# A decoder layer's mixer output projection: column blocks taken in pairs, with seven products in three of eight chunk pairs

## The chip, the cores and the metric

The kernel runs on one NeuronCore of a Trainium2 chip. Its time is the device time of one execution in microseconds. Work is spread over TensorE (PE, matrix products; its weight loads are listed as PEld), VectorE (DVE, elementwise), ScalarE (ACT, casts and activations), GpSimd (POOL, some elementwise work and a DMA queue) and SyncE (SP, the queue that loads the weights).

## The reference

One decoder layer on 256 tokens of width 2048, all in float32:

```python
x = x + 0.5 * swiglu(rms_norm(x, g1), w_gate, w_up, w_down)          # width 5632
h = rms_norm(x, g2); p = h @ w_in
merged = gate_attn * (y_attn @ w_proj_attn) + gate_rwkv * (y_rwkv @ w_proj_rwkv)
x = x + merged @ w_out                                               # 2048 x 2048
x = x + cross_attention(rms_norm(x, g3), rms_norm(mem, g4))          # 256 memory rows
x = x + 0.5 * swiglu(rms_norm(x, g5), ...)
return rms_norm(x, g6)
```

`y_attn` is a sliding-window attention, `y_rwkv` an RWKV-7 recurrence. The change lies in the line `x = x + merged @ w_out`.

## The kernel before, in words

**Float32 in two parts.** A matmul operand v is split into a rounded part `hi` (float32r) and the rest `lo = v - hi`. A product is three matmuls: hi·hi, hi·lo and lo·hi (`times`, L413 to L419). Activations are split once. Weights are split as they come: `load` (L321) brings a unit (two chunks of 128 rows by 512 columns, 512 KB) on SyncE's queue, `split_unit` (L338) casts `hi` on ScalarE (L344) and subtracts `lo` on VectorE (L345). In the mixer the raw weights have four buffers of one unit (tag `raw` of the pool `w`); in the feed-forwards they come in double units from a pool of their own, eight units ahead. `hi` and `lo` have three buffers each.

**Single blocks and pairs.** `product` (L399) computes one column block of 512: for each unit 12 matmuls (two chunks, two halves of the tokens, three parts). `product_pair` (L474) computes two column blocks together, one *item* (two units, one of each block) at a time. Over two chunks and two token halves these are eight products. In some items they become seven, by combinations in the manner of Strassen and Winograd: of the weights (L371 to L374, four subtractions into two further tiles, which `two_parts`, L348, splits into `thi` and `tlo`) and of the activations (`combinations`, L428: `chi` and `clo`). The sums then come out as p1 to p7 in banks of PSUM: p6 and p7 in the two banks that transposes use (`tr`), p1, p3, p5 in `mm`, p2, p4 and a further q in `acc`. The caller's `first`, `middle` and `out` combine them. The feed-forwards use pairs: (0, 2, 4) of eight items in gate and up, (2, 4, 6) or (2, 4) in down (`SEVEN`, `SEVEN_DOWN`). The mixer and the cross-attention use single blocks.

**Order of the work.** The weights come in the order of `weight_plan` (L97). `next_item` (L376) loads and divides an item and those after it, up to two units ahead (`AHEAD`). Side work is written as generators in an `Interleave` (L52): groups such as `feat` (transposes of a finished block and its split), `chain` (the recurrence), `norm`, `ew` and `mem`; each `tick` between products takes a step of each group. A scheduler then orders each engine's instructions by its own planned times, and adds waits on buffers.

**The stages around the change.** For each of four column blocks the kernel multiplies `yr` by `w_proj_rwkv` (L1394 to L1402); VectorE multiplies by the gate (`gl`, L1400), GpSimd adds the attention's share (`ml`, L1401), and `merged` transposes and splits the block into `mt`. Then the output projection (L1414 to L1424): for each block `product(mt, w_out)`, VectorE adds to the residual `x2` (L1421, read from `x1d` by GpSimd's queue, L1418), and the norm of that block (`n3.block`, L633) is spawned. Beside it `memory` (L1407) loads four blocks of the memory (L1410), and norms and transposes them. All the mixer's larger tiles share a ring of 23 (`t4`); the recurrence's smaller tiles (`xs`, `p`, `d`, `sm`, `yq`, `nt`, `bk`, `sq`) lie beside it in the same pool `mx` until the mixer ends.

Of the kernel before, what the change touches and what calls it, by code (L numbers as in the profile page):

```python
# [7 lines left out]
F32 = mybir.dt.float32  # L8
# [7 lines left out]
P = 128  # L16
# [21 lines left out]
SEVEN, SEVEN_DOWN = (0, 2, 4), ((2, 4, 6), (2, 4))  # L38

# [93 lines left out]
def decoder_layer(ctx: ExitStack, tc: tile.TileContext, a: dict, out: bass.AP):  # L133
# [185 lines left out]
    at = {"item": 0, "product": 0, "pool": None}  # L319
# [28 lines left out]
    def two_parts(v, e):  # L348
        sp = at["pool"]
# [3 lines left out]
        dve.tensor_tensor(lo[:], v[:], f32(hi[:]), ALU.subtract)  # L353
        return hi, lo

    def divide(i):
# [13 lines left out]
        t = [wp.tile([P, KU, 512], F32, tag="raw", name="raw", bufs=4) for _ in range(2)]  # L370
# [58 lines left out]
    def combinations(sp, x: Act, seven, name, ready=lambda: True, early=True):  # L429
# [8 lines left out]
        def work():  # L438
# [3 lines left out]
            for q in pairs:  # L442
                while not {2 * q, 2 * q + 1} <= x.done:
                    yield
                t = wp.tile([P, KU, 512], F32, tag="raw", name="raw", bufs=4)
# [31 lines left out]
    def product_pair(x: Act, c, w, first, middle, out):  # L477
# [28 lines left out]
        for q in range(nk // KU):  # L506
            k = KU * q
            if q in seven:
                bg.until(lambda: c["done"] and (q > min(seven) or not bg.groups["feat"][1]))
                g, u, s = next_item()  # L510
# [13 lines left out]
                if end:  # L524
                    middle(b)
                continue
# [46 lines left out]
    def down(sp, h: Act, c, w, xs):  # L573
# [3 lines left out]
        def half(x_, v):  # L577
            dve.scalar_tensor_tensor(x_, v, 0.5, x_, ALU.mult, ALU.add)
# [6 lines left out]
        def middle(b):  # L585
# [5 lines left out]
            half(xs[0][1], u2[:])  # L591

# [179 lines left out]
    with tc.tile_pool(name="mx", bufs=1, reuse_waits="tile") as sp:  # L772
# [5 lines left out]

        def act_tiles(name, n):
# [130 lines left out]
        def shifted(tok, cols, mus, outs, name):  # L910
            for q in range(0, len(cols), 2):
                n = len(cols[q : q + 2])
                b = feat(tok, cols[q : q + 2])
                p = sp.tile([P, 2, T + 1], F32, tag="p", name="p", bufs=2)
# [3 lines left out]
                d = sp.tile([P, 2, T], F32, tag="d", name="d", bufs=2)  # L918
# [19 lines left out]
        xs = sp.tile([P, 3, T], F32, name="xs")  # L938
# [237 lines left out]
        def small(name, tag="sm", bufs=6):  # L1176
            return sp.tile([P, 2, P], F32, tag=tag, name=name, bufs=bufs)
# [25 lines left out]
        def pairs(h, q):  # L1203
# [3 lines left out]
            y = yq[h, q] = sp.tile([P, 2, T], F32, tag="yq", name="yq", bufs=3)  # L1207
# [7 lines left out]
            for c in range(2):  # L1215
# [30 lines left out]
                nt = sp.tile([P, 4, P], F32, tag="nt", name="nt", bufs=2)  # L1246
# [18 lines left out]
                if c == 0:  # L1265
# [5 lines left out]
                    bk = sp.tile([P, 4, P], F32, tag="bk", name="bk", bufs=2)  # L1271
# [51 lines left out]
        def finish(h, i):  # L1323
# [6 lines left out]
            g2 = sp.tile([P, 2, 2 * P], F32, tag="yq", name="g2", bufs=3)  # L1330
# [4 lines left out]
            sq = sp.tile([P, 2 * T], F32, tag="sq", name="sq", bufs=1)  # L1335
# [58 lines left out]
        for n in range(4):  # L1394
# [7 lines left out]
            bg.spawn("feat", merged(m, n))  # L1402
# [4 lines left out]
        def memory():  # L1407
            for n in range(4):
# [3 lines left out]
                yield from nm_.block(n, s)  # L1412

        x2 = []  # L1414
        for n in range(4):
            s = t4("x2", (P, 2, 512))
            x2.append(s)
            pool.dma_start(s[:], blk(x1d, n))  # L1418
            po = product(mt, W["w_out"])
            for t in range(2):  # L1420
                dve.tensor_tensor(s[:, t, :], po[t][:], s[:, t, :], ALU.add)  # L1421
            bg.spawn("feat", n3.block(n, s))
            if n == 0:
                bg.spawn("mem", memory())  # L1424

# [154 lines left out]
```

## Time and profile before

| | us |
|---|---|
| median of 3 runs | 2251.83 (2251.02 to 2252.10) |
| the profiled execution, its own time | 2252.57 |
| its span in the trace | 2250.8 |
| output projection: first to last matmul on `mt` | 1339.8 to 1435.8 |

The page gives busy times by engine, 40 slices of the span, the DMA queues, the chain that ended last, and groups of instructions by line. In a group stand the line, the engine, the operation, output and input, the shape, the count, the busy time and the mean duration in ns, and after the last bar the idle time before and what ended it. Times in a timeline are start and duration in us from the span's start; `x3` means three instructions merged in one row. A row of stretches has the length, then the busy time of PE, PEld, DVE, ACT and POOL with the number of instructions, the granted clock, the DMA share and GB/s. Matmuls are pipelined, so a matmul's duration is longer than the distance to the next one.

### The profile page before, as it was taken

What the parts mean: (1) busy time and instruction counts of PE and PEld (TensorE: products, weight loads), DVE (VectorE), ACT (ScalarE), POOL (GpSimd) and SP (SyncE); (2) the same over time, 40 slices, a digit from 0 to 9 for tenths busy, and PEclk for the clock granted to TensorE, in tenths of its full rate; (3) what the DMA queues carried; (4) which work ended last, traced back from release to release, by engine and by line L of the source; (5) the groups of instructions that cost most, each with busy time, mean ns of one, the idle gap of its engine ahead of it and who ended that gap; (6) DMA issues with size and microseconds to landing.
All of it is one profiled execution on the core that took longest, in us unless ns stands there. A gap on an engine that the chain in (4) does not pass through costs nothing.

```text
span 2250.8 us, 28046 instructions
## 1 busy us (share of the span) xinstructions
PE 2235.2 (99%) x10617; PEld 1840.3 (82%) x10617; DVE 1782.0 (79%) x2279; ACT 1226.5 (54%) x1601; POOL 132.6 (6%) x192
## 2 busy tenths in 40 slices
PE   9999999999999999999999999999999999999998
PEld 7888888888888877788888888888888888888886
DVE  7898988998989476887534566557998988998987
ACT  6555555555556467444444446556555555554554
POOL 1000000000001000301220040001000000000002
PEclk9999999999999999999999999999999999999999
DMA  7555555556556544676523476548565565555564
GB/s 263 187 201 201 197 203 202 193 190 216 192 188 205 163 142 150 201 223 212 166 77 109 163 261 227 186 159 284 185 213 187 195 210 194 190 209 200 189 207 147
DMA packets 219143, 432.49 MB, mean 192 GB/s; under 512 B 14107, under 2 KB 16384, under 8 KB 219008
## 3 DMA queue, kind: packets, MB, share of 16 engines
q1 hardware_dynamic: 210432, 404.78, 53.3%
q0 software_dynamic: 8112, 25.12, 3.5%
q8 instruction: 83, 1.36, 0.2%
q10 hardware_dynamic: 464, 0.79, 0.1%
q14 instruction: 52, 0.43, 0.1%
HBM read 417.56 MB, written 13.11 MB: 191 GB/s over the span
## 4 chain that ended last, share of the span: by engine, by line
PE 94%; DVE 3%; DMA 1%; issue 1%; POOL 1%; ACT 0%; SPq 0%; POOLq 0%; DVEq 0%; ACTq 0%
PE acc L417 19%; PE acc L418 19%; PE acc L419 19%; PE mm L419 8%; PE mm L418 8%; PE mm L417 8%; PE tr L605 2%; PE tr L418 2%; PE tr L419 2%; PE tr L417 2%; PE mm L1254 1%; DVE lo L345 1%; PE tr L1190 1%; DMA raw<-in_w_out_dram 0%; PE mm L844 0%
## 5 line engine op out<-in xcount | busy, mean ns | idle before, releaser
L345 DVE TENSOR_TENSOR lo<-raw,hi 128x1024 fp32r<-128x1024 f32 (+1 forms) x770 | 894.5, 1163 | 336.6 <-ACT hi L344 334.4
L344 ACT CAST hi<-raw 128x1024 fp32r<-128x1024 f32 (+1 forms) x770 | 759.3, 997 | 734.7 <-PE acc L419 519.6
L417 PE MATMUL acc<-hi,xhi 128*128 128x512 f32 (+1 forms) x1196 | 474.3, 397 | 2.4 <-ACT xhi L632 1.9
L418 PE MATMUL acc<-lo,xhi 128*128 128x512 f32 (+1 forms) x1196 | 464.8, 389 | 0.0
L419 PE MATMUL acc<-hi,xlo 128*128 128x512 f32 (+1 forms) x1196 | 464.1, 388 | 0.0
L417 PEld LDWEIGHTS acc<-hi,xhi 128*128 128x128 f32 x1196 | 225.0, 188 | 51.4 <-issue 4.0
L419 PEld LDWEIGHTS acc<-hi,xlo 128*128 128x128 f32 x1196 | 224.5, 188 | 46.9 <-DVE xlo L633 1.0
L418 PEld LDWEIGHTS acc<-lo,xhi 128*128 128x128 f32 x1196 | 224.9, 188 | 45.3 <-issue 1.7
L352 ACT CAST thi<-raw 128x1024 fp32r<-128x1024 f32 x172 | 178.9, 1050 | 60.4 <-DVE raw L373 46.5
L353 DVE TENSOR_TENSOR tlo<-raw,thi 128x1024 fp32r<-128x1024 f32 x172 | 208.3, 1220 | 0.7 <-ACT thi L352 0.4
L417 PE MATMUL mm<-hi,xhi 128*128 128x512 f32 x380 | 149.3, 393 | 0.0
L419 PE MATMUL mm<-hi,xlo 128*128 128x512 f32 x380 | 148.2, 390 | 0.0
L418 PE MATMUL mm<-lo,xhi 128*128 128x512 f32 x380 | 148.2, 390 | 0.0
L418 PE MATMUL acc<-lo,hhi 128*128 128x512 f32 x372 | 145.6, 391 | 0.8 <-DVE lo L345 0.8
L419 PE MATMUL acc<-hi,hlo 128*128 128x512 f32 x372 | 145.6, 391 | 0.0
L417 PE MATMUL acc<-hi,hhi 128*128 128x512 f32 x372 | 144.9, 390 | 0.0
L419 PEld LDWEIGHTS mm<-hi,xlo 128*128 128x128 f32 x380 | 71.3, 188 | 14.8
L418 PEld LDWEIGHTS mm<-lo,xhi 128*128 128x128 f32 x380 | 71.4, 188 | 14.5
L417 PEld LDWEIGHTS mm<-hi,xhi 128*128 128x128 f32 x380 | 71.4, 188 | 14.5
L418 PEld LDWEIGHTS acc<-lo,hhi 128*128 128x128 f32 x372 | 69.9, 188 | 15.5 <-DVE lo L345 1.2
L417 PEld LDWEIGHTS acc<-hi,hhi 128*128 128x128 f32 x372 | 69.9, 188 | 14.3
L419 PEld LDWEIGHTS acc<-hi,hlo 128*128 128x128 f32 x372 | 69.9, 188 | 14.0
(392 smaller groups left out, 3511.9 us busy)
## 6 DMA issues: line engine op xcount, KB each, us to landing
raw<-in_ffn_w_up_dram SPq DMA_DIRECT2D x88, 1024.0 KB, 5.4
raw<-in_ffn_w_down_dram SPq DMA_DIRECT2D x88, 1024.0 KB, 5.1
raw<-in_ffn_w_gate_dram SPq DMA_DIRECT2D x84, 1024.0 KB, 5.1
raw<-in_w_in_dram SPq DMA_DIRECT2D x136, 512.0 KB, 3.5
raw<-in_w_out_dram SPq DMA_DIRECT2D x32, 512.0 KB, 4.5
raw<-in_w_proj_attn_dram SPq DMA_DIRECT2D x16, 512.0 KB, 3.9
raw<-in_w_proj_rwkv_dram SPq DMA_DIRECT2D x16, 512.0 KB, 5.7
raw<-in_w_cross_kv_dram SPq DMA_DIRECT2D x16, 512.0 KB, 3.6
```

The lines of the kernel that those rows point to most:

```text
L344: at["hi"] = act.copy(hi[:, s], raw[:, s])
L345: at["lo"] = dve.tensor_tensor(lo[:, s], raw[:, s], f32(hi[:, s]), ALU.subtract)
L352: act.copy(hi[:], v[:])
L353: dve.tensor_tensor(lo[:], v[:], f32(hi[:]), ALU.subtract)
L417: pe.matmul(o, xh, hi, start=first, stop=False, **how)
L418: pe.matmul(o, xh, lo, start=False, stop=False, **how)
L419: pe.matmul(o, xl, hi, start=False, stop=last, **how)
L605: pe.transpose(b[:, o : o + P], tok[:, t, col : col + P], ident[:])
L1190: pe.matmul(b[e][:, o : o + P], x1[r, j, cs_], x2[r, j, cs_], start=True, stop=True)
L1254: pe.matmul(vb[:, (o + k) * P : (o + k + 1) * P][:, r], lhs(k, e), rhs[:, k, r], start=first and k + e == 0, stop=True, **ek,)
```

## The change

- `w_out` is taken in two pairs of column blocks, (0, 512) and (1024, 1536), with seven products in items 0, 2 and 3 of eight (`SEVEN_OUT`). The units of both blocks are loaded in turns.
- The recurrence's smaller tiles move to a pool `rk` of their own. When the first block of `w_proj_rwkv` is done, the pool is closed and a pool `out` opened in its room, for `chi`, `clo`, `thi`, `tlo` and the sums `u`. The raw sums of weights and activations go into the ring `t4` instead of the ring of the raw weights.
- The pair's results are combined by `down` with the factor 1.0 in place of 0.5. In `middle`, after the last item with seven products, it now spawns what waits in `c["next"]`: in the first pair the transposes of the last merged block, in the second the norms of the first two residual blocks. The norms of the last two follow the second pair.
- The residual blocks are loaded two at a time ahead of each pair. `memory` takes no step while a pair is in its items with seven products (`at["sevens"]`).

```diff
+SEVEN_OUT = (0, 2, 3)
...
-    for n in range(4):
-        yield w["w_out"], 0, KD, n * 512, 512
+    for n in (0, 1024):
+        yield (w["w_out"], w["w_out"]), 0, KD, (n, n + 512), SEVEN_OUT
...
+        if len(ends) == 1:
+            for q in range(nk // KU):
+                items.append(((len(units), len(units) + 1), q in n))
+                units += [(v, k0 + KU * q, c, 512) for v, c in zip(w, c0)]
+            continue
...
-        t = [wp.tile([P, KU, 512], F32, tag="raw", name="raw", bufs=4) for _ in range(2)]
+        t = [at["sums"]() for _ in range(2)]
...
-    def down(sp, h: Act, c, w, xs):
+    def down(sp, h: Act, c, w, xs, factor=0.5):
...
             half(xs[1][1], u3[:])
             half(xs[0][1], u2[:])
+            while c.get("next"):
+                bg.spawn("feat", c["next"].pop(0))
...
+        chains = ExitStack()
+        rp = chains.enter_context(tc.tile_pool(name="rk", bufs=1, reuse_waits="tile"))
+        at["sums"] = lambda: t4("sums", (P, KU, 512))
...
-            bg.spawn("feat", merged(m, n))
+            if n == 0:
+                bg.until(lambda: not any(bg.groups[e][1] for e in ("chain", "norm", "ew")))
+                chains.close()
+                op = chains.enter_context(tc.tile_pool(name="out", bufs=1, reuse_waits="tile"))
+                at["parts"] = op
+                cm = combinations(op, mt, SEVEN_OUT, "c", early=False)
+                cm["next"] = []
+            if n < 3:
+                bg.spawn("feat", merged(m, n))
+            else:
+                cm["next"].append(merged(m, n))
...
-                yield from nm_.block(n, s)
+                steps = nm_.block(n, s)
+                while True:
+                    while at["sevens"]:
+                        yield
+                    if next(steps, bg) is bg:
+                        break
+                    yield
...
-        for n in range(4):
-            s = t4("x2", (P, 2, 512))
-            x2.append(s)
-            pool.dma_start(s[:], blk(x1d, n))
-            po = product(mt, W["w_out"])
-            for t in range(2):
-                dve.tensor_tensor(s[:, t, :], po[t][:], s[:, t, :], ALU.add)
-            bg.spawn("feat", n3.block(n, s))
+        for n in (0, 2):
+            for m in (n, n + 1):
+                s = t4("x2", (P, 2, 512))
+                x2.append(s)
+                pool.dma_start(s[:], blk(x1d, m))
             if n == 0:
                 bg.spawn("mem", memory())
+            down(op, mt, cm, W["w_out"], [[x2[n + i][:, t, :] for i in range(2)] for t in range(2)], 1.0)
+            if n == 0:
+                cm["next"] += [n3.block(m, x2[m]) for m in range(2)]
+        for m in (2, 3):
+            bg.spawn("feat", n3.block(m, x2[m]))
+        chains.close()
+        at["sums"] = sums
```

More of the change, by code (lines that the diff above doesn't have):

```diff
@@ L318, in decoder_layer, with sums @@
     raws, parts = {}, {}
-    at = {"item": 0, "product": 0, "pool": None}
+    at = {"item": 0, "product": 0, "pool": None, "sevens": False}
+    def sums():
+        return wp.tile([P, KU, 512], F32, tag="raw", name="raw", bufs=4)
+    at["sums"] = sums
     def load(u, pieces=None):
@@ L348, in two_parts @@
     def two_parts(v, e):
-        sp = at["pool"]
+        sp = at["pool"] or at["parts"]
         hi = sp.tile([P, KU, 512], F32R, tag="thi" + e, name="thi")
@@ L444, in work @@
                     yield
-                t = wp.tile([P, KU, 512], F32, tag="raw", name="raw", bufs=4)
+                t = at["sums"]()
                 v = t[:, 0].rearrange("p (k t n) -> p k t n", k=2, t=2)
@@ L509, in product_pair @@
                 bg.until(lambda: c["done"] and (q > min(seven) or not bg.groups["feat"][1]))
+                at["sevens"] = True
                 g, u, s = next_item()
@@ L525, in product_pair @@
                     middle(b)
+                    at["sevens"] = False
                 continue
@@ L913, in shifted @@
                 b = feat(tok, cols[q : q + 2])
-                p = sp.tile([P, 2, T + 1], F32, tag="p", name="p", bufs=2)
+                p = rp.tile([P, 2, T + 1], F32, tag="p", name="p", bufs=2)
                 pool.memset(p[:, :, 0:1], 0.0)
@@ L917, in shifted @@
                 yield
-                d = sp.tile([P, 2, T], F32, tag="d", name="d", bufs=2)
+                d = rp.tile([P, 2, T], F32, tag="d", name="d", bufs=2)
                 pool.tensor_tensor(d[:, :n], p[:, :n, :T], p[:, :n, 1:], ALU.subtract)
@@ L936, in halves @@
             return x[:].rearrange("p c (b t) -> p (c b) t", b=2)
-        xs = sp.tile([P, 3, T], F32, name="xs")
+        xs = rp.tile([P, 3, T], F32, name="xs")
         xwa, xg = xs[:, 0, :], xs[:, 1:, :]
@@ L1176, in small @@
         def small(name, tag="sm", bufs=6):
-            return sp.tile([P, 2, P], F32, tag=tag, name=name, bufs=bufs)
+            return rp.tile([P, 2, P], F32, tag=tag, name=name, bufs=bufs)
         def masked(h, js, which):
@@ L1206, in pairs @@
             js = (2 * q, 2 * q + 1)
-            y = yq[h, q] = sp.tile([P, 2, T], F32, tag="yq", name="yq", bufs=3)
+            y = yq[h, q] = rp.tile([P, 2, T], F32, tag="yq", name="yq", bufs=3)
             if q == 0:
@@ L1245, in pairs @@
                         )
-                nt = sp.tile([P, 4, P], F32, tag="nt", name="nt", bufs=2)
+                nt = rp.tile([P, 4, P], F32, tag="nt", name="nt", bufs=2)
                 act.copy(nt[:], b[:].rearrange("p (k t) -> p k t", k=4))
@@ L1329, in finish @@
             f2 = slice((4 * h + 2 * i) * P, (4 * h + 2 * i + 2) * P)
-            g2 = sp.tile([P, 2, 2 * P], F32, tag="yq", name="g2", bufs=3)
+            g2 = rp.tile([P, 2, 2 * P], F32, tag="yq", name="g2", bufs=3)
             pool.memset(g2[:96, 1, :], 0.0)
@@ L1334, in finish @@
             y = yq[h, i][:].rearrange("p c t -> p (c t)")
-            sq = sp.tile([P, 2 * T], F32, tag="sq", name="sq", bufs=1)
+            sq = rp.tile([P, 2 * T], F32, tag="sq", name="sq", bufs=1)
             act.activation(sq[:], y, AF.Square)
```

5 lines of the change are left out of this document (3 added, 2 removed).

## The prediction

> **What bounds the kernel now.** I read the page's busy times and slices first, then stretches of the output projection (about 1328 to 1436 us) beside a dense stretch of the first feed-forward, then instructions in order of time.
>
> ```profile
> span 2250.8 us, 28046 instructions
> ...
> PE 2235.2 (99%) x10617; PEld 1840.3 (82%) x10617; DVE 1782.0 (79%) x2279; ACT 1226.5 (54%) x1601; POOL 132.6 (6%) x192
> ...
> PE   9999999999999999999999999999999999999998
> ...
> DVE  7898988998989476887534566557998988998987
> ```
>
> TensorE is busy from end to end, so a matmul less is time less, if nothing new holds it up. VectorE is the second limit: nine tenths where pairs of column blocks with seven products run (both ends), five to six in the middle, where this change lies.
>
> ```profile
> core 0: us, PE busy (x) PEld busy (x) DVE busy (x) ACT busy (x) POOL busy (x), PEclk, DMA share, GB/s
> 1328.00:1436.00 108.00, 107.02 (x506) 87.91 (x505) 66.01 (x81) 59.40 (x96) 13.43 (x13) 1.00 0.63 217
> 480.00:540.00 60.00, 60.00 (x266) 49.68 (x266) 56.73 (x69) 32.48 (x34) 0.00 (x0) 1.00 0.57 194
> ```
>
> In the projection VectorE works 66 of 108 us. The second row shows what the same scheme does elsewhere: VectorE 56.7 of 60 us (94.5%), and TensorE does not stop. The clock is 1.00 in both, so no gain or loss is sought there.
>
> **The change part by part.** *Matmuls removed.* A block pair over one chunk pair takes 8 products of 3 matmuls; with seven it takes 21 instead of 24. Three of eight chunk pairs, two block pairs: 6 x 3 = 18 matmuls fewer. A matmul's listed 0.39 us overlaps the next one's; what counts is start to start.
>
> ```profile
> 1351.59 0.39 PE L417 MATMUL acc<-hi,mthi 128*128 128x512 f32 x1
> ...
> 1354.31 0.39 PE L417 MATMUL acc<-hi,mthi 128*128 128x512 f32 x1
> ```
>
> These two rows are 12 matmuls apart: 2.72 / 12 = 0.227 us. So 18 x 0.227 = **-4.1 us**, a seven item takes 21 x 0.227 = 4.8 us of TensorE and a plain one 5.4 us.
>
> *A stall removed.* After the first column block TensorE waits for the residual sum before it can transpose it.
>
> ```profile
> 1363.60 0.39 PE L419 MATMUL acc<-hi,mtlo 128*128 128x512 f32 x1
> 1364.70 0.33 PE L605 MATMUL tr<-ident,x 128*128 128x128 f32 x1 [0.71 <-DVE x L1421]
> 1365.30 0.55 PE L605 MATMUL tr<-ident,x 128*128 128x128 f32 x3 [0.27 <-DVE x L1421]
> ```
>
> A step of 1.10 where 0.23 is usual, and of 0.60 where transposes follow each other at 0.11 (three in the last row's 0.55, the last of them 0.33 long): 0.9 + 0.5 = 1.4 us lost. The new order puts these transposes half a pair later: **-1.4 us** (bound: 0, if the transfers described below bring it back). Best case of both: -5.5 us, 0.24%.
>
> *VectorE's new work.* One seven item in the feed-forward, with two 128x1024 splits of a neighbouring item among its own:
>
> ```profile
> 533.97 0.69 DVE L371 TENSOR_TENSOR raw<-raw,raw 128x512 f32<-128x512 f32 x1 [1.24 <-DMA raw<-in_ffn_w_up_dram]
> 534.58 1.22 DVE L345 TENSOR_TENSOR lo<-raw,hi 128x1024 fp32r<-128x1024 f32 x1
> 535.71 0.69 DVE L372 TENSOR_TENSOR raw<-raw 128x512 f32<-128x512 f32 x1
> 536.31 0.68 DVE L373 TENSOR_TENSOR raw<-raw,raw 128x512 f32<-128x512 f32 x1
> 537.03 0.69 DVE L374 TENSOR_TENSOR raw<-raw,raw 128x512 f32<-128x512 f32 x1
> 537.64 1.22 DVE L345 TENSOR_TENSOR lo<-raw,hi 128x1024 fp32r<-128x1024 f32 x1
> 538.78 1.22 DVE L353 TENSOR_TENSOR tlo<-raw,thi 128x1024 fp32r<-128x1024 f32 x1
> 539.91 1.22 DVE L345 TENSOR_TENSOR lo<-raw,hi 128x1024 fp32r<-128x1024 f32 x1
> 541.05 1.22 DVE L353 TENSOR_TENSOR tlo<-raw,thi 128x1024 fp32r<-128x1024 f32 x1
> 542.18 0.69 DVE L345 TENSOR_TENSOR lo<-raw,hi 128x512 fp32r<-128x512 f32 x1
> ```
>
> Start to start a 128x512 takes 0.60 and a 128x1024 takes 1.14. From 533.97 to 542.18 + 0.60 are 8.8 us; less two neighbouring splits (2.3) a seven item costs VectorE 6.5 us against TensorE's 4.8; a plain item costs 2.3 against 5.4. Chunk pairs 2 and 3 are neighbours: 13 us of VectorE stand against 9.5 of TensorE. In the feed-forward a plain item always lies between (0, 2, 4).
>
> ```profile
> L455 DVE TENSOR_TENSOR raw<-raw 128x128 f32<-128x128 f32 x22 | 6.3, 284 | 0.1
> L633 DVE SCALAR_TENSOR_TENSOR xlo<-tr,gains,xhi 128x256 fp32r<-128x256 f32 x16 | 7.6, 482 | 3.8 <-ACT xhi L632 3.8
> ```
>
> In sum the change adds to VectorE 24 subtractions of 0.60 and 12 second parts of 1.14; 6 splits of 1.14 become 6 of 0.60; three combinations of the activations (two of 0.60 and four small ones, 0.28 listed and at 0.2 apart, an estimate: the list of the longer ones also shrinks by 0.08) cost 6; evictions go from 8 to 24 of 0.60. That is 14.4 + 13.7 - 3.2 + 6 + 9.6 = 40.5 us. With the 66.0 of before it makes 106.5; less 3.1, since some 35 splits that stand alone now will overlap (1.23 listed, 1.14 apart), and less 1.9 for the four norm instructions of the third residual block (0.48 each), which now fall behind the projection: 101.5 us. TensorE would need 108 - 5.5 - 1.1 (eight transposes that fall behind it with them) = 101.4. VectorE would have to work without a gap, where the densest row above shows 94.5%. At that density the stretch takes 101.5 / 0.945 = 107.4, against 106.9 for the same work before: +0.5. So from above nothing is won.
>
> *From below, by the order of the instructions.* These rows are the start:
>
> ```profile
> 1327.73 1.28 DVE L1400 TENSOR_TENSOR gl<-acc,gl 128x512 f32<-128x512 f32 x2
> ...
> 1339.57 1.28 DVE L1400 TENSOR_TENSOR gl<-acc,gl 128x512 f32<-128x512 f32 x2
> 1341.05 1.67 DVE L345 TENSOR_TENSOR lo<-raw,hi 128x1024 fp32r<-128x1024 f32 x1 [0.19 <-ACT hi L344]
> ```
>
> Between the two evictions, 11.8 us, the changed order has 13.8 us of VectorE: the first eviction (1.2), two combinations' rest (2.6), three splits (3.4), two transposed halves (1.2), and of the first seven item 2.5 + 2.3 + 0.6. Its first second-part comes some 0.4 us after TensorE has done what it can without it, and the last gate eviction, behind it on VectorE, holds the bank of one product 0.2 more: **+0.6** (0 to 2.0, all that VectorE is behind). Then VectorE does gate (1.2), item 1 (2.3) and 4.8 of item 2, whose second part is there just when TensorE comes to it: whatever delays VectorE up to there is paid in full. One such delay is in the last row: 1.67 instead of 1.23, while GpSimd adds.
>
> ```profile
> 1340.35 3.52 POOL L1401 TENSOR_TENSOR ml<-gl,ml 128x512 f32<-128x512 f32 x2 [7.64 <-DVE gl L1400]
> 1343.82 0.72 POOL L1418 DMA_DIRECT2D x<-x1d  x1
> 1344.54 2.89 POOL L1410 DMA_DIRECT2D mem<-in_mem_dram  x4
> ...
> L1401 POOL TENSOR_TENSOR ml<-gl,ml x8: 1281/1293/2270, 1304.7 to 1341.6; 128x512 f32<-128x512 f32 x8
> ```
>
> Now VectorE's work beside those 3.5 us is without gaps and mostly of two SBUF inputs. Least price 0.44 (that row), most 2.6 (two adds of 1.28, the shortest of the last row, shut out whole): **+1.0**, nearer the row. The page "SBUF — State Buffer" of the Trainium skill, section "SBUF: two separate sides", says that a VectorE operation with two SBUF inputs and a GpSimd operation that reads SBUF lock each other out for a whole instruction; by that rule the term would be 2.6 and the time 2252.9 us, and the one stretched row agrees with it in kind.
>
> *Item 3 of each pair.* On ScalarE the cast of item 4's first weight stands ahead of item 3's first `thi`, so a weight that lands late holds up item 3. There are four buffers of one unit each and no more, and that unit's is free after item 2's fourth subtraction. From there TensorE waits 1.2 for item 2's second part, has 17 matmuls of item 2 (3.9) and 3 of item 3 (0.7): 5.8 us until it wants `thi`. Meanwhile come the landing and two casts.
>
> ```profile
> L344 ACT CAST hi<-raw 128x1024 fp32r<-128x1024 f32 x672 | 698.3, 1051 | 674.5 <-PE acc L419 479.8 <-PE mm L419 148.6 <-issue 9.0
> ...
> raw<-in_w_out_dram SPq DMA_DIRECT2D x6, 512.0 KB, 9.0
> ...
> DMA to landing us min/median/max: 3.5/4.5/10.7
> ```
>
> With casts of 1.05 the stall is the landing + 2.1 - 5.8. The row of 9.0 is for issues from 1344 to 1362 us, when six transfers of GpSimd's queue share the engines; the last row is for the whole projection. In the new order that queue issues two residual blocks and one memory block before its last adds, two memory blocks right behind them (beside items 2 and 3), one after item 3 and the last residual blocks later still: two at that place instead of six. A landing of 4.5 costs 0.8, of 9.0 it costs 5.3; I take 5.2, nearer the median: **+1.5**. Second pair: its banks wait for the first pair's evictions (0.3), then items 2 and 3 with landings at the median (0.6 each): **+1.5** (0 to 5.6).
>
> Sum: -4.1 - 1.4 + 0.6 + 1.0 + 1.5 + 1.5 = -0.9. With +0.5 from above I take -0.5. Against its own time of 2252.6 us (the profiled execution, 0.7 above the median of the runs) that is 2252.1; against the median of 2251.8 it is **2251.3 us**.
>
> What costs nothing: the first products' share and everything after the cross-attention keep their order; the later norm blocks run in a product where VectorE needs 2.3 per 5.4 us; the new pools' waits are on tiles long finished. Pausing the memory's norm while the sevens hold both transpose banks only moves it.
>
> **The rivals.** *It runs as in the feed-forward.* VectorE gets ahead far enough, and only the 0.6 at the start is paid: -4.9, 2246.9 us. For it: 94.5% with a full TensorE. Against it: there no two seven items are neighbours, and weights are loaded in double units, eight ahead instead of four.
>
> *The weights come late (slower).* If the landings are the 9.0 us above beside the first pair's items 2 and 3 (5.3) and halfway, 6.8, beside the second's (3.1 and 0.9 for the rest), and the 1.4 stall's cause stays: -4.1 + 0.6 + 1.0 + 5.3 + 3.1 + 0.9 = +6.8, 2258.6 us. It decides from the point where the new stalls reach 5.5 us, landings of about 5.3 us in both pairs (1.6 + 1.6 beside 0.6 + 1.0 + 0.9). For it: 128 x 1024 units at one per 2.4 us is 220 GB/s of weights alone. Against it: the burst is split up. The page "DMA: Bandwidth & Descriptors", section "Queues, rings and completion order", says that a DMA engine takes turns between the queues that have work; by that rule a unit lands in twice its usual time while the other queue has work, 9.0 us as an estimate from the median of 4.5, and the row of 9.0 beside GpSimd's six transfers agrees.
>
> *It does not do what it says.* The built program has exactly 18 matmuls of 512 columns fewer, so I give this nothing.
>
> **How the numbers follow.** A measurement of this kernel tells about 0.2%, 4.5 us, from no change. Partly eaten gain, my forecast: 0.44, with 2247.5 to 2256 for itself. Hidden as in the feed-forward: 0.24; even its best, -5.5, barely passes 0.2%. Late weights: 0.32, since every unknown of mine adds to the stalls and they carry over from item to item. The range goes from near the best case, 2246.8, to 2258.0.
>
> **What would show it.** Right: 18 matmuls fewer; VectorE over 90% busy from 1328 us to the projection's end; TensorE's stops at `tlo`, `thi` or `lo` of items 2 and 3, some 5 us in all; no stop before the residual's transposes. Wrong on the fast side: no stops at items 2 and 3. Wrong on the slow side: ScalarE's casts ended by weights' landings of 6 us and more, or stops of TensorE outside the projection.

## The result and the profile after

| | before | after |
|---|---|---|
| median (range), us | 2251.81 (2251.02 to 2253.03) | 2255.53 (2254.05 to 2256.28) |
| the profiled execution, its own time | 2252.57 | 2254.32 |
| its span | 2250.8 | 2252.6 |

The changed kernel takes 1.0015 of the time before, 95% interval 1.0009 to 1.0021: 3.7 us slower, where 0.5 us faster was forecast. It lies inside the predicted range (2246.8 to 2258.0) and inside the 0.2% that the prediction called no change, but the interval is clear of 1, so the loss is real. The profiled executions show only 1.75 us of it: the one after lies 1.2 us below the median of its runs, the one before 0.8 above. Two further profiled executions of the changed kernel are among the experiments.

The page of the changed kernel, busy times:

```profile
span 2252.6 us, 28109 instructions
...
PE 2233.5 (99%) x10599; PEld 1835.6 (81%) x10599; DVE 1822.0 (81%) x2349; ACT 1238.4 (55%) x1618; POOL 133.8 (6%) x192
```

18 matmuls fewer, and VectorE's busy time 40.0 us up where 40.5 had been worked out. Stretches, the output projection:

```profile
core 0: us, PE busy (x) PEld busy (x) DVE busy (x) ACT busy (x) POOL busy (x), PEclk, DMA share, GB/s
1328.00:1436.00 108.00, 103.70 (x473) 81.46 (x472) 100.19 (x135) 67.32 (x104) 14.27 (x15) 1.00 0.64 220
```

VectorE went from 66.0 to 100.2 of 108 us (93%), TensorE from 1.0 to 4.3 us idle. The instructions in order of time (start, duration; in brackets the idle time before and what ended it) show where TensorE stops:

```profile
1333.30 0.39 PE L430 MATMUL acc<-hi,yrhi 128*128 128x512 f32 x1
1334.65 0.50 PE L431 MATMUL acc<-lo,yrhi 128*128 128x512 f32 x1 [0.96 <-DVE lo L358]
1334.99 0.39 PE L432 MATMUL acc<-hi,yrlo 128*128 128x512 f32 x1
...
1353.24 0.40 PE L431 MATMUL mm<-lo,mthi 128*128 128x512 f32 x1
1354.23 0.50 PE L431 MATMUL tr<-tlo,chi 128*128 128x512 f32 x1 [0.59 <-DVE tlo L366]
...
1358.66 0.39 PE L430 MATMUL mm<-hi,chi 128*128 128x512 f32 x1
1359.96 0.73 PE L430 MATMUL tr<-thi,chi 128*128 128x512 f32 x2 [0.91 <-ACT thi L365]
...
1376.82 0.48 PE L432 MATMUL mm<-hi,mtlo 128*128 128x512 f32 x1
1377.52 0.50 PE L430 MATMUL acc<-hi,mthi 128*128 128x512 f32 x1 [0.22 <-ACT mthi L627]
...
1392.88 0.39 PE L430 MATMUL acc<-hi,mthi 128*128 128x512 f32 x1
1393.75 0.50 PE L430 MATMUL acc<-thi,mthi 128*128 128x512 f32 x1 [0.47 <-DVE x L593]
```

A stop is the step from start to start less the usual 0.23: 1.12 us still in `w_proj_rwkv`, 0.76 at item 2 of the first pair, 1.07 at item 3, 0.47 at the last merged block's first product, 0.64 at the second pair's start. With the shorter ones (0.32 and 0.38 ahead of items 0 and 1, 0.22 ahead of item 2, 0.22 at 1375, 0.37, 0.31 and 0.46 in the second pair) they make 6.3 us, twelve stops in all. Steps that are longer by less than 0.2 each add 1.4 more than before; 1.2 of these are the step right behind each stop, 0.34 in place of 0.23 (third row). The stop of 1.4 us ahead of the residual's transposes is gone. In sum -4.1 - 1.4 + 6.3 + 1.4 = +2.2. Outside the stage TensorE lost 0.7 less than before, which leaves +1.5 against the span's +1.8.

What VectorE does ahead of some of these stops:

```profile
1329.35 1.78 DVE L462 TENSOR_TENSOR sums<-mthi,mtlo 128x512 f32<-128x512 f32 x1
...
1331.86 1.40 DVE L470 TENSOR_TENSOR sums<-sums 128x128 f32<-128x128 f32 x1
...
1345.31 4.19 DVE L358 TENSOR_TENSOR lo<-raw,hi 128x1024 fp32r<-128x1024 f32 x2
...
1356.59 0.69 DVE L384 TENSOR_TENSOR sums<-raw 128x512 f32<-128x512 f32 x1 [0.68 <-DMA raw<-in_w_out_dram]
```

and GpSimd beside it:

```profile
1328.91 1.67 POOL L1423 TENSOR_TENSOR ml<-gl,ml 128x512 f32<-128x512 f32 x1 [7.99 <-DVE gl L1422]
...
1331.82 1.28 POOL L1423 TENSOR_TENSOR ml<-gl,ml 128x512 f32<-128x512 f32 x1 [0.57 <-DVE gl L1422]
...
1344.89 3.52 POOL L1423 TENSOR_TENSOR ml<-gl,ml 128x512 f32<-128x512 f32 x2 [8.95 <-DVE gl L1422]
1348.36 1.45 POOL L1442 DMA_DIRECT2D mem<-in_mem_dram  x2
```

In this execution VectorE's instructions that begin while one of GpSimd's additions runs are stretched: 1.78 where the others of this shape take 0.68, 1.40 for 0.28, and 4.19 for two splits that take 2.35 elsewhere (a row of another kernel below). That is 1.1 + 1.1 + 1.8 = 4.0 us. An instruction that is already under way when the addition begins keeps its time: `clo` at 1328.75 took its 0.68, and it was the addition that took 1.67 in place of 1.28. The last row of the first fence is the other candidate: VectorE has nothing to do and waits for item 3's second weight, whose transfer was issued just behind two of the memory's:

```profile
mem<-in_mem_dram POOLq DMA_DIRECT2D x1, 512.0 KB, 7.2
raw<-in_w_out_dram SPq DMA_DIRECT2D x1, 512.0 KB, 7.0
```

(transfers issued from 1349.3 to 1349.8 us, the last number the us to landing).

### The profile page after: what moved, and what is told of

It reads as the page before. It is cut to its first block, busy times and chain, and to the rows that moved or that the text cites. A ratio compares the mean times of both kernels' runs of the same rounds, so it can differ in the third digit from the quotient of the medians.

```text
span 2252.6 us, 28109 instructions
## 1 busy us (share of the span) xinstructions
PE 2233.5 (99%) x10599; PEld 1835.6 (81%) x10599; DVE 1822.0 (81%) x2349; ACT 1238.4 (55%) x1618; POOL 133.8 (6%) x192
## 4 chain that ended last, share of the span: by engine, by line
PE 94%; DVE 3%; DMA 1%; issue 1%; ACT 1%; SPq 0%; POOL 0%; POOLq 0%; DVEq 0%; ACTq 0%
PE acc L430 18%; PE acc L431 18%; PE acc L432 18%; PE mm L432 8%; PE mm L431 8%; PE mm L430 8%; PE tr L622 2%; PE tr L431 2%; PE tr L430 2%; PE tr L432 2%; PE mm L1276 1%; DMA raw<-in_w_out_dram 1%; DVE lo L358 1%; PE tr L1212 1%; PE mm L866 0%
```

## The experiments

There are four theories. *Shut-out*: GpSimd's additions hold up VectorE, and the stops follow. *Late weights*: GpSimd's transfers share the DMA engines with the weights, and with four buffers a late unit reaches TensorE. *Density*: VectorE simply has too much to do where seven items are neighbours. *Pair form*: the pairs, their banks and evictions cost the time even without seven products. Times are medians; the kernel before, on the same chip, stood at 2251.8 to 2252.2.

**Pairs without seven products.** `SEVEN_OUT` empty in the plan, `p2` to `p5` summed over all eight items, the same places for the spawns and the pause.

```diff
-        yield (w["w_out"], w["w_out"]), 0, KD, (n, n + 512), SEVEN_OUT
+        yield (w["w_out"], w["w_out"]), 0, KD, (n, n + 512), ()
```

> The changed kernel with pairs of column blocks, the same order of spawning and pausing, but eight products in every item (18 matmuls more, 4.1 us; no combinations). Shut-out theory and density rival alike: VectorE has slack, no stops at items 2 and 3 and none at the start; the 1.4 us ahead of the residual's transposes stay away, 0.7 come at the second pair's start: 2251.8 - 1.4 + 0.7 = 2251.1, less than with seven products. Rival, the pair form itself (units of two blocks in turns, banks, evictions) costs the time: 2253.5 or more.

Measured: 2250.75 (2250.47 to 2251.07), ratio 0.9995, 0.9987 to 1.0004. In the projection's stretch TensorE is busy throughout:

```profile
1328.00:1436.00 108.00, 108.00 (x509) 89.26 (x508) 66.45 (x79) 58.65 (x90) 13.41 (x13) 1.00 0.67 220
```

The pair form costs nothing; by itself it brings about 1.1 of the 1.4 us of the removed stall. So the six items with seven products, which take 4.1 us of matmuls away, cost 4.8 us on balance and nearly 9 us gross.

**GpSimd's additions left out, and put on VectorE.**

```diff
-                pool.tensor_tensor(m[:, t, :], g[:, t, :], m[:, t, :], ALU.add)
+                (pool if n < 2 else dve).tensor_tensor(m[:, t, :], g[:, t, :], m[:, t, :], ALU.add)
```

> The changed kernel with the additions `ml` of the last two blocks on VectorE instead of GpSimd; nothing is left out. Shut-out theory: VectorE gets 4 x 0.60 = 2.4 us more to do and is shut out 4.0 us less, 1.6 net, so about 1.5 us less, 2254.0. Density rival: 2.4 us more work in the same stretch, 1 to 2.4 us more, 2256.5 to 2258.

> The changed kernel without GpSimd's additions `ml` for the last two blocks of `w_proj_rwkv`: the attention's share is left out there, and the transposes take `gl` instead, so they still wait for the gate. Shut-out theory (GpSimd's additions hold up VectorE's operations beside them by 1.1 + 1.1 + 1.8 = 4.0 us at 1329, 1331 and 1345 us, and the stops at 1333, 1340, 1346, 1353 us and part of the one at 1358 us follow from that): these stops, 1.1 + 0.3 + 0.4 + 1.0 = 2.8 us, and half of the last one's 1.1 go; 3.2 us less than the changed kernel's 2255.5, so 2252.3. Rival, VectorE's own density (items 2 and 3 are neighbours and it has 13 us of work in 9.5): the stops at items 2 and 3 stay at 1.0 + 1.1, 1 us less at most, 2254.5. Rival, late weights: no change, 2255.5.

Measured: on VectorE 2252.97 (2252.14 to 2253.53), ratio 1.0005; left out 2254.38 (2253.66 to 2256.10), ratio 1.0014. Both are puzzling as they stand: less work is the slower of the two, and the time with the additions left out is the one that density foretold. With the additions on VectorE its two splits do run in their usual time:

```profile
1346.19 2.35 DVE L358 TENSOR_TENSOR lo<-raw,hi 128x1024 fp32r<-128x1024 f32 x2
```

and the stop of 1.12 in `w_proj_rwkv` is gone, in both runs; item 0's grows from 0.32 to 0.56, and to 1.20 with the additions left out. But GpSimd's queue has also lost what it waited for, so its transfers moved. Five of them went out at 1321 to 1324 instead of 1330 to 1335, and item 0's weights landed after 9.7 to 10.9 us instead of 3.5 to 4.0. With the additions on VectorE a memory block went out at 1345.36 in place of two at 1348 to 1349. Where the additions are left out, one goes out at 1342.39, just ahead of the weight of item 2, which lands after 6.9 us; TensorE stops 1.5 us for it at 1351. From 1354.6 to 1358.0 the granted clock then was 0.5, TensorE's step 0.43 in place of 0.23, which cost another 1.5 us in the profiled execution (2255.70). So neither run separates the two causes, which the expectations had overlooked.

**The memory's transfers, later.** `memory` is spawned behind item 3 of the first pair; then, since that did not hold the transfers, each of its tiles also takes one column from a residual block before its load.

```diff
+                pool.tensor_copy(s[:, 0, 0:1], x2[1][:, 0, 0:1])
                 pool.dma_start(s[:], blk(W["mem"], n))
```

> The changed kernel with `memory` spawned behind item 3 of the first pair, so that none of its transfers runs beside the first four items. Rival, late weights: the units that landed in 8.0 and 9.4 us at the start and in 7.0 us ahead of item 3 land in about 4.5; the stops at 1346 (0.4) and 1358 us (1.1) go, 1.5 less, 2254.0. Shut-out theory: the stops at 1333, 1340 and 1353 us stay, 0.7 us less at most, 2254.8. Both: up to 1 us more if the memory's norm is late for the cross-attention.

> The changed kernel with the memory's transfers really held back: each of its tiles first takes one column from a residual block as it stands behind item 3 of the first pair (a copy of 128 x 1 on GpSimd), so that the four transfers come after it. In the run before, spawning them later only moved three of them beside item 3, where a unit then landed in 9.3 us and TensorE stopped 0.9 + 2.3 us. Late-weights theory (GpSimd's transfers share the DMA engines, with four buffers a unit late by 3 us reaches TensorE): the stop ahead of item 3 (1.1 in the changed kernel's profile, up to 3.2 with three transfers) goes, and with it the spread between executions: 2255.5 - 1.1 to 2 = 2253.5 to 2254.4, the runs within 1 us of each other. Shut-out theory alone: item 2's stop of 0.8 and the start's stay, item 3's stays too, since VectorE was late in freeing the buffers: 2255.5.

Spawned later: 2256.34 (2254.47 to 2257.41), no faster; ratio 1.0019, 1.0010 to 1.0028. The later spawn freed GpSimd's queue at the start, and three transfers now go out together at 1348.5 us, beside item 3:

```profile
1358.58 0.39 PE L430 MATMUL acc<-hi,mthi 128*128 128x512 f32 x1
1359.74 0.49 PE L430 MATMUL mm<-hi,chi 128*128 128x512 f32 x1 [0.78 <-ACT hi L357]
1362.22 0.50 PE L430 MATMUL tr<-thi,chi 128*128 128x512 f32 x1 [1.98 <-ACT thi L365]
```

```profile
raw<-in_w_out_dram SPq DMA_DIRECT2D x1, 512.0 KB, 9.3
```

There are three transfers instead of two (two ahead of this unit and one right behind), 9.3 us instead of 7.0 to landing, and stops of 0.9 and 2.2 ahead of item 3. Shortly behind them, from 1363.6, the granted clock was again 0.5 for 3.4 us and TensorE's step 0.43. So the total of this run does not tell a longer wait from a lower clock. Really held back, the time is 2262.08 (2261.30 to 2264.40): the stop ahead of item 3 falls to 0.3 as late weights say, but the order of TensorE's instructions is fixed when the kernel is built, and its transposes of the memory now stand ahead of products while their data is still on the way:

```profile
1379.30 1.09 PE L624 MATMUL tr<-ident,mem 128*128 128x128 f32 x4 [4.83 <-DMA mem<-in_mem_dram]
```

The granted clock was 0.5 for 6.8 us from there on. The total says nothing on the theories; the place does. The same with the additions on VectorE:

> Both at once: the memory's transfers held back, and the last two blocks' additions on VectorE. If shut-out and late weights are the two causes, the start's and the first pair's stops nearly all go (4.1 of them in the changed kernel's profile, less up to 1 for the 2.4 us more on VectorE) and the second pair's 1.8 stay: 2252.97 with the additions on VectorE alone, less 1 to 1.5: 2251.5 to 2252. If VectorE's density is the cause, it stays at 2253.

Measured: 2259.45 (2254.86 to 2263.93). It missed for the same reason (2.2 us ahead of the memory's transposes, 1.8 later on), and these stops are those of the profiled execution, 2254.86, the lowest of the five. Its stop at item 2 is gone, that at item 3 is 1.15.

**The changed kernel again.** No edit; what differs between its executions?

> The changed kernel again, unaltered, for another profiled execution: the first one (2254.3 us) lies at the low end of its runs (2254.0 to 2256.3). Late weights: an execution of 2255.5 or more shows the same stops at the start and at item 2, and a longer one ahead of item 3, with the unit issued at 1349.5 us landing in 9 us instead of 7.0. Shut-out or density alone: all stops grow a little, or none does and the time lies outside the projection.

> As the run before it: a third profiled execution of the changed kernel. Late weights: its time follows the stop ahead of item 3; below 2254.5 with one of about 1 us, above 2255.4 with one of 2 to 3 us.

Measured: 2255.17 and 2256.13. The stop ahead of item 3 is 1.07 in the first profiled execution (2254.32), 1.87 and 1.97 in these; the unit issued at 1349.5 to 1349.9 landed after 7.0, 8.0 and 8.0 us. The slowest of the three:

```profile
1358.99 0.39 PE L430 MATMUL mm<-hi,chi 128*128 128x512 f32 x1
1361.18 0.50 PE L430 MATMUL tr<-thi,chi 128*128 128x512 f32 x1 [1.81 <-ACT thi L365]
...
1357.98 0.69 DVE L384 TENSOR_TENSOR sums<-raw 128x512 f32<-128x512 f32 x1 [1.75 <-DMA raw<-in_w_out_dram]
...
1359.14 1.05 ACT L357 CAST hi<-raw 128x1024 fp32r<-128x1024 f32 x1 [0.53 <-DMA raw<-in_w_out_dram]
1360.09 1.04 ACT L365 CAST thi<-sums 128x1024 fp32r<-128x1024 f32 x1
```

VectorE, said to be the bottleneck, waits 1.75 us for item 3's second weight. But the wait that ends last is ScalarE's: the cast of item 4's first weight starts when that weight lands, and item 3's `thi` stands behind it. VectorE has the sums for `thi` ready 0.2 us before ScalarE turns to it (0.2 in the second execution, 0.4 in the first). The unit of item 4, issued at 1353.1 to 1353.4, landed after 4.7, 5.5 and 5.6 us in the three executions. The other stops are the same within 0.2 us in two of the three and shift by 0.6 between items 1 and 2 in the third. The time follows item 3 only in part: 0.9 of the 1.8 us between the first and the last execution lies elsewhere, 0.2 to 0.4 each ahead of the projection, in the second pair and behind the projection, and between the second and the third, 1 us apart, item 3 differs by 0.1.

**One memory block used four times.** The other three blocks' data are left out: their transfers at 1348, 1349 and 1363 us are gone, TensorE's order stays.

```diff
-                s = t4("mem", (P, 2, 512))
-                pool.dma_start(s[:], blk(W["mem"], n))
+                if n == 0:
+                    s = t4("mem", (P, 2, 512))
+                    pool.dma_start(s[:], blk(W["mem"], n))
```

> The changed kernel with one of the memory's four blocks loaded and used four times (the other three blocks' data are left out), so that the transfers issued at 1348 and 1349 us, beside item 3, and at 1363 us are gone and all else stays. Late-weights theory: the unit issued at 1349.5 us lands in 4 to 5 us instead of 7.0 to 8.0, the stop ahead of item 3 falls from 1.1 to 2.0 to about 0.3 (as in the run with the memory held back), and the spread between executions with it: 2255.5 - 1.6 = 2253.9; the stops at the start and at item 2 (0.8 to 1.0) stay. If only VectorE's lateness counts, the time stays at 2255.5.

Measured: 2252.89 (2252.59 to 2253.38), 2.6 us less than the changed kernel and 0.9 above the kernel before on the same chip (ratio 1.0004, 0.9995 to 1.0013). The unit of item 3 and TensorE's step there:

```profile
raw<-in_w_out_dram SPq DMA_DIRECT2D x1, 512.0 KB, 4.4
```

```profile
1358.96 0.39 PE L430 MATMUL mm<-hi,chi 128*128 128x512 f32 x1
1359.45 0.74 PE L430 MATMUL tr<-thi,chi 128*128 128x512 f32 x2
```

The stop is 0.27 instead of 1.07 to 1.97; item 4's unit landed after 3.6 us. The stops at the start (1.12) and at item 2 (0.76) are there as before, with VectorE as stretched as ever, and item 1's is 0.66. The second pair gained too, 0.9 us of stops: the residual blocks for it went out at 1363 and 1377 instead of 1384 and 1392, so not beside its first items (0.64 became 0.17 there). By the profiled stops the gain is 0.8 to 1.7 at item 3 and 0.9 in the second pair. Its total lies 1 us below what was expected, by that second place.

**Both cures.**

> The same with the last two blocks' additions on VectorE. If the two causes add up: no stop at the start or at item 2 beyond 0.8 in all, and ahead of item 3 the 1.1 that four buffers leave with landings of 4.8 us (4.8 + 2.1 - 5.8): 2252.97 less 0 to 1, 2252.0 to 2253.0, with the second pair's 1.8 of stops as they were. If item 3's stop goes too, the buffers are not to blame: 2251.5.

Measured: 2252.67 (2251.54 to 2253.59), 0.2 less than the run before, no difference beside this spread. The stops at the start and at item 2, 1.12 + 0.76, are gone. Those at items 0 and 1 are 0.57 and 0.85 (0.31 and 0.66 in the run before), 1.4 in all where 0.8 was expected, and one ahead of item 3 is back:

```profile
1357.29 0.40 PE L430 MATMUL mm<-hi,chi 128*128 128x512 f32 x1
1358.66 0.50 PE L430 MATMUL tr<-thi,chi 128*128 128x512 f32 x1 [0.97 <-ACT thi L365]
...
1356.61 1.05 ACT L357 CAST hi<-raw 128x1024 fp32r<-128x1024 f32 x1 [1.00 <-DMA raw<-in_w_out_dram]
```

ScalarE waits for item 4's first weight with item 3's `thi` behind it, the mechanism that the prediction described. That unit was issued at 1352.26 and landed after 4.3 us, and TensorE, now earlier, wanted `thi` 5.3 us after the issue instead of 5.8: 4.3 + 2.1 - 5.3 = 1.1 by the prediction's formula, 1.14 measured. So the two cures do not add. A VectorE that comes earlier only brings TensorE earlier to the weight, which the four buffers let go out no sooner. Shut-out is real, but moving the additions to VectorE, which has 2.4 us of work more by it, gains nothing clear once the transfers are gone; what the additions cost beside the transfers these runs do not separate. Density as the whole cause falls: with the transfers gone VectorE has the same work, and the time is 2.6 us less. Its share in the stops that are left is open.

**Where the seven items lie.** Other sets, among them only in the second pair.

```diff
-SEVEN_OUT = (0, 2, 3)
+SEVEN_OUT = ((0, 2), (0, 2, 4))   # spaced
+SEVEN_OUT = ((), (0, 2, 4))       # second pair only
+SEVEN_OUT = ((), (0, 2, 4, 6))    # four in the second pair
+SEVEN_OUT = ((4,), (0, 2, 4))     # one late in the first
+SEVEN_OUT = ((3, 5), (1, 3, 5))   # late in the first
```

(Each line is from another run's edit, with the run named behind it. In the last two the last merged block is transposed at the first pair's start.)

> Seven products in items 0 and 2 of the first pair and 0, 2 and 4 of the second: 15 matmuls fewer than before, 0.7 us of TensorE more than the changed kernel, and no two seven items are neighbours. Density rival: the stops at item 3 of both pairs (1.1 + 0.5) and most of the second pair's others go: 2255.5 + 0.7 - 2 = 2254.2 or less. Shut-out and late weights: the start's and item 2's 2.8 us stay, and item 3 is plain but its weights land as late; its first product needs only one of them: 2255.5 + 0.7 - 1 = 2255.2.

> The first pair with eight products everywhere (as in the run without seven products), the second with seven in items 0, 2 and 4: 9 matmuls fewer than before. Places theory (the start of the projection is where VectorE is shut out and where GpSimd's transfers run; the second pair has neither, and its sevens are no neighbours): 2250.75 - 2.05 + 0.6 (bank at the second pair's start) + 0.2 = 2249.5. Density rival (a seven item always costs the single-unit ring more than it saves): 2251 or more.

> The first pair with eight products everywhere, the second with seven in items 0, 2, 4 and 6: 12 matmuls fewer than before. Places theory: 0.7 less than with three of them, 2249.82 - 0.7 = 2249.1, plus up to 0.8 if the first two residual blocks' transposes, now behind item 6, push the norms past the projection: 2249.1 to 2249.9.

> Seven products in item 4 alone of the first pair, past the memory's transfers and GpSimd's additions, and in 0, 2 and 4 of the second; the last merged block is transposed at the first pair's start. 12 matmuls fewer than before. Places theory: 2249.82 (second pair alone) - 0.7 + 0.3 = 2249.4. If a seven item in the first pair costs more than its 0.7 us wherever it lies: 2250.5 or more.

> Seven products in items 3 and 5 of the first pair and 1, 3 and 5 of the second, 15 matmuls fewer than before; the last merged block is transposed at the first pair's start. Places theory: item 3 of the first pair begins near 1357 us, where the weights behind the memory's transfers still land late in the run with sevens in the second pair alone (8.8 us for the unit issued at 1348), so up to 1.5 us there: 2249.82 - 1.4 + 0 to 1.5 = 2248.4 to 2249.9, and 2 us more if the memory's norm, paused longer, is late. Density rival: 2251 or more.

*Spaced*: 2255.75 (2254.97 to 2257.65). No two seven items are neighbours, and still the stops up to item 2 come to 2.5 us (2.8 in the changed kernel) and the second pair's to 1.6 (1.8): their spacing is not what governs these. The total decides nothing, since 2.4 us are lost at 1361 ahead of the memory's transposes. These need a bank that VectorE has yet to empty, and VectorE's evictions stand behind a split whose weight, issued between three of the memory's transfers at 1349 to 1350, landed after 9.1 us. *Second pair only*: 2249.82 (2249.06 to 2251.44), ratio 0.9991, 0.9982 to 1.0000, where 2249.5 was expected: 2.1 us below the kernel before and the best of all, though its interval reaches no change.

```profile
1328.00:1436.00 108.00, 107.99 (x508) 88.39 (x507) 86.98 (x114) 64.43 (x100) 14.17 (x13) 1.00 0.69 226
```

TensorE does not stop, though the units issued in the first pair beside the memory's transfers land as late as ever:

```profile
raw<-in_w_out_dram SPq DMA_DIRECT2D x3, 512.0 KB, 7.5
```

(issued from 1348 to 1356 us). A late unit cost nothing here, where the items are plain; in the changed kernel it had to pass three subtractions and a cast before the first product. In the second pair two residual blocks go out, at 1379 and 1388, and a unit behind one landed after 6.3 us, but TensorE lost only 0.3 us there.

*Four in the second pair*: 2257.49, where 2249.1 to 2249.9 was expected. The residual's norms now start behind item 6, and the transposes of the memory and of the residual fall into the next product one upon the other, with 3.4 us of stops from 1452 to 1456 and the granted clock at 0.5 for 3.4 us behind them; 2.1 us more go ahead of item 4's products at 1407 to 1410:

```profile
1454.72 0.63 PE L628 MATMUL tr<-ident,mem 128*128 128x128 f32 x4 [1.66 <-issue]
```

*One late in the first*: 2251.15, 1.3 more than without it, where 2249.4 was expected. Its p6 and p7 need the two transpose banks, of which the memory's norm has one until VectorE has read it:

```profile
1370.48 0.47 PE L430 MATMUL tr<-thi,chi 128*128 128x512 f32 x1 [1.49 <-DVE melo L650]
```

*Late in the first*: 2257.43, where 2248.4 to 2249.9 was expected. 4.1 us of it go at 1347 us to transposes of the memory whose block is still under way, and behind them the granted clock was 0.5 for 3.4 us; the total says nothing on the theories.

## Why the prediction was wrong

The prediction's terms beside the stops of the three profiled executions of the changed kernel (us; the steps and the times outside are against the profiled execution before):

| | forecast | first | second | third |
|---|---|---|---|---|
| matmuls and stall removed | -5.5 | -5.5 | -5.5 | -5.5 |
| start (`w_proj_rwkv`, item 0) | 0.6 | 1.4 | 1.4 | 1.5 |
| GpSimd's additions (items 1 and 2) | 1.0 | 1.4 | 1.5 | 1.4 |
| item 3 | 1.5 | 1.1 | 1.9 | 2.0 |
| second pair | 1.5 | 1.8 | 1.4 | 2.1 |
| last merged block, 1375 to 1377 | 0 | 0.7 | 0.7 | 0.7 |
| steps slightly longer than usual | 0 | 1.4 | 1.2 | 1.4 |
| outside the stage | 0 | -0.7 | -0.2 | 0 |
| sum | -0.9 | 1.6 | 2.4 | 3.6 |
| change of the span | -0.5 | 1.8 | 2.6 | 3.6 |

**Matmuls removed, -4.1, and the stall removed, -1.4**: right. 18 matmuls went, the stop ahead of the residual's transposes is gone, and the pairs alone were 1.1 us faster.

**VectorE's new work**: 40.5 worked out, 40.0 measured. The bound from above (+0.5) was not what decided: VectorE reached 93%, but with waits of its own for weights in between. Going from -0.9 to -0.5 for that bound's sake has no sum behind it: with +0.5 from above alone it would have been 2252.3 us.

**The start, +0.6** (0 to 2.0): 1.44 (1.12 + 0.32). Its larger part came one stage earlier than the prediction looked, in the last block of `w_proj_rwkv`. The step counted the work between two evictions and let GpSimd's additions of the block before run beside it free of charge; each cost VectorE 1.1 us there. With these additions off GpSimd that stop is gone; item 0's of 0.56 and 1.20 in those two runs stand behind weights that landed late.

**GpSimd's additions, +1.0** (0.44 to 2.6), "nearer the row": VectorE was stretched 1.8 by the last two and 2.2 by the two before. The stops that go with the last two are 0.38 + 0.22 + 0.76 = 1.4 us, nearer 1.0 than 2.6. The page "SBUF — State Buffer" of the Trainium skill, section "SBUF: two separate sides", by whose rule the term was 2.6, agrees better with the stretching than the single row: the earlier two stretched a VectorE instruction of two SBUF inputs by 1.10 and 1.12, the last two by 1.84 together.

**Item 3, +1.5**: right in mechanism and about in size, the size by a lucky guess. The formula (landing of item 4's first weight + 2.1 - 5.8) gives 1.0, 1.8 and 1.9 for the landings of 4.7, 5.5 and 5.6 us; the stops were 1.07, 1.87 and 1.97. With three transfers in a row it gives 6.9 + 2.1 - 5.8 = 3.2, as measured (0.9 + 2.2). The landing of 5.2 was taken "nearer the median" between 4.5 and 9.0 with no reason, and came out near the mean of the three. Not foreseen was that item 3's own second weight lands later still, after 7.0 to 8.0 us, so that VectorE is only 0.2 to 0.4 us from being the last wait. The page "DMA: Bandwidth & Descriptors" of the Trainium skill, section "Queues, rings and completion order", says that a DMA engine takes turns between the queues that have work. An estimate from it is twice the time, 8.8 from the 4.4 without those transfers; the 7.0 to 8.0 measured here come near it. The slower rival (2258.6) had the right mechanism at too large a size: two units of the first pair were late, the one that counted by 1.1 to 2.0 us, not all of them at 9.0.

**The second pair, +1.5**: 1.8 (0.64, 0.37, 0.31, 0.46). It is about right in sum. Not foreseen was why it is as much: two residual blocks go out beside its first items, and with these earlier the pair's stops were 0.9 less.

**The step that failed** is the sum: it holds four waits, and what stands around them was put at nothing without a reason. That is 0.7 us at 1375 to 1377, where the change itself has chunks 12 to 15 transposed and cast just ahead of their use, and 1.2 to 1.4 us of longer steps, mostly the one behind each stop. Together they are 2.0 us. The next largest is the start, 0.8 to 0.9 more than its 0.6 through additions that it took as free. The terms that were priced came to 6.2 us in the mean of the three executions where 4.6 was forecast; with the 2.0 that makes 8.2 us of losses against 5.5 of gain, less 0.3 outside the stage. The rest of the 3.7 us is that the profiled execution before lay 0.8 above its median, and those after 0.3 below theirs on average; no trace shows where.

What a cure brought is another list than what the sum left out. The memory's and the residual's transfers beside the items with seven products are worth 2.6 us, somewhat more than half of the 4.8 us to the pairs without seven products, but without them the kernel is still no faster than before (2252.89).

Open: what VectorE's sheer load has in the stops that are left; what the additions left out would bring with the transfers gone, which was not run; whether a fifth and sixth weight buffer would let both cures add, which was not tried; and where the small differences between executions outside item 3 come from.

## What to carry to other kernels

Seven products for eight pay only where the weights are certain to be there: such an item passes a landed weight through three subtractions and a cast before its first matmul, and late transfers that the four buffers hid in plain items reached TensorE here. Look first for other queues' transfers, GpSimd's work and shared banks at the place, and put the scheme where there are fewest: here three seven items in the second pair (2249.8) beat six in both (2255.5). Count the stops as well as their lengths, since each brings a longer step behind it. A cure's worth is known only by taking it beside the others: with the transfers gone, moving the additions that stretch VectorE by 4 us off GpSimd gained 0.2, since the next wait stood right behind it.

## What the runs showed of the hardware

Where a 128x512 addition on GpSimd (1.28 us alone) met a VectorE instruction with two inputs in SBUF, one of the two grew by up to the other's length: VectorE's from 0.28 to 1.40 and from 0.68 to 1.78, two splits from 2.35 to 4.19 beside two additions, and in the third execution of the changed kernel the addition from 1.28 to 2.27. Small instructions suffer most in proportion. A 512 KB unit landed after 4.4 us without transfers of GpSimd's queue just ahead, 7.0 to 8.0 with two ahead, 9.3 with two ahead and a third right behind. Behind a stop the step after TensorE's next 512-column matmul took 0.34 us in place of 0.23. In the profiled executions of five runs a granted clock of 0.5 followed stops of 1.5 to 5 us, for 3.4 us (6.8 with the memory held back), with steps of 0.43 us: about 1.5 us lost in 3.4; after stops of 2.0 and 2.4 us in others it stayed at 1.00. The spread between executions is no measure of late transfers: it was 2.2 us in the changed kernel, 0.8 with three of the memory's transfers gone, but 2.0 with the same three gone and the additions moved, and 0.6 without seven products with all four of them there.
